# Modulation weights of stage 0 split by GpSimd, with products issued two pieces behind

## The chip, the cores and the metric
One core of one Trainium2 chip (trn2). The metric is the device time of one launch in microseconds (us), the median of the runs shown. TensorE is called PE, its weight loads PEld, VectorE DVE, ScalarE ACT, GpSimd POOL, SyncE SP, as in the profile; a q behind a name is that engine's instruction queue.

## The reference, cut to what matters
One step of a small diffusion backbone on 512 latent and 128 context tokens of width 1024, in fp32. Layer 0 mixes by pooling, layer 1 by retention; each is followed by an MLP. Every sub-layer has a norm with shift, scale and gate that come from the conditioning vectors:

```python
mod = (jax.nn.silu(cond) @ w_ada[i] + b_ada[i])[:, None, :]
sh_a, sc_a, g_a, sh_m, sc_m, g_m = jnp.split(mod, N_MOD, axis=-1)
h = rmsnorm(x, norm_mix_w[i]) * (1 + sc_a) + sh_a
mix = pool_mixer(h, pool_w[j], pool_b[j], pool_scale[j], grid)
x = x + g_a * mix
h = rmsnorm(x, norm_mlp_w[i]) * (1 + sc_m) + sh_m
x = x + g_m * sq_relu_mlp(h, mlp_w1[i], mlp_w2[i])
```

`cond` has two rows here (c for the latent tokens, c_ctx for the context), so that a modulation is a product of 2 vectors of 1024 with a 1024x1024 matrix: 4 MB of weights for few multiplications.

## The kernel before
All tokens stand side by side as 640 columns, with the features on partitions (`xall`, eight tiles of 128 features). An fp32 matmul with full accuracy is made of three faster ones: each operand is split into a high part `hi` of type fp32r and the rest `lo` (`split`, line 144: ACT casts `hi`; line 145: a TENSOR_TENSOR subtracts, on DVE unless `sub` names another engine), and `mm3` (lines 205 to 207) adds hi*hi, hi*lo and lo*hi.

**Stage 0** is layer 0 up to its MLP. Five of layer 0's six modulations are made in it, in the order 1, 0, 2, 4, 3 (`ada`, called with `MODES`). A modulation has eight pieces, two halves of 512 columns with four pieces of 256 rows each; so there are 40, and piece 17 is the first of modulation 2, 25 the first of 4, 33 the first of 3. Two pieces come by one DMA of 1 MB into a `wst` buffer. The letter of `MODES` says how a piece is taken:
- `p`: whole; two fp32 products on PE (line 283, `ps<-wst,c`; each is two MATMUL records of the profile), straight from the `wst` buffer;
- `v`: split, the low part on DVE; four fp32r products (`ps<-whi,chl` and `ps<-wlo,chl`);
- any other letter (`g`): split, the low part on POOL.

`LAG` is how many pieces the products stand behind: `queue` holds the pieces that are split and not yet multiplied, and `issue` takes the oldest once more than `LAG` are in it. When a half is complete, line 287 copies the sum from PSUM (ACT), line 293 turns it by transposes on PE, line 294 adds it up on DVE (`mod`), and lines 304 and 414 finish the modulation. `PLAN` says after which step of the other work how many pieces are taken. That other work is:
- `pooled(d)` for eight feature tiles: transposes (621, 622), window sums (630, 632), the scaled token n (637, ACT), the difference df (638 and 639, DVE: 638 reads PSUM and `iv`, 639 reads df and n), its split into `h{d}h` and `h{d}l` (144 ACT, 145 DVE). For every second d, `group` splits four token tiles (`t<-xt`), makes `pm` (601) and loads `iv` (596, on ACT's queue);
- line 659: x gets the bias of the pooling (ACT, 16 pieces of work); it needs modulation 2;
- the pool adds, `pool_add(n, h)`: six matmuls with the split pool weights (two `whi`/`wlo` pairs, which stay in use until the end), `xall` (line 500, DVE), the square (435, ACT) and its sum (447 DVE, or 455 PE);
- the norm ahead of the MLP: `rsqrt` (lines 150 to 159, DVE) for each half of the tokens, then line 487 (DVE) and 489 (ACT), which give the first operand of the MLP's first matmul.

`whi` and `wlo` have four buffers each, for the pieces, the pool weights and the MLP's weights. The order on each engine is set by a scheduler when the kernel is built; each engine then runs its queue in order.

Of the kernel before, what the change touches and what calls it, by code (L numbers as in the profile page):

```python
# [46 lines left out]

MODES = ("pvvv vvvv", "vvvv vvvv", "vpvp vpvp", "ppvp ppvp", "ppvp ppvp")  # L50
MODE5 = "s s"
PLAN = ("a2 l a4 v a5 a5 w0 a2 w1 a2 w2 a2 w3 a2 w4 a2 w5 a2 w6 a2 w7",
        "a1", "a1", "a1", "a1", "a1", "a1", "a1", "a1")
LAG = 1
FIRST = "x x x x x"
LATE = (False, True)
TURN = 5
# [53 lines left out]
def hybrid_kernel(ctx: ExitStack, tc: tile.TileContext, x_prompt, x_sample, state_ret, c, c_ctx, w_ada, b_ada,  # L111
# [6 lines left out]
    def nm(s):  # L118
        uid[0] += 1
        return f"{s}_{uid[0]}"  # L120
# [280 lines left out]
    def stepper(gen):  # L401
        def step(n=1, until=None):
            while n if until is None else until not in ready:
                try:
                    next(gen)
                except StopIteration:
                    return
                n -= 1
        return step
# [141 lines left out]
    with tc.tile_pool(name="pool", bufs=1) as pp:  # L551
        extra[:] = [(wst, 2), (pp, 3), (pp, 3), (wst, 2), (pp, 3)]
        win_sb = pp.tile([128, W_N], F32, name="win_sb")
        room[1] = lambda: pp.tile([128, 1024], F32, tag="acc", name=nm("acc"), bufs=1)
        astep = stepper(ada([(0, m, modes) for m, modes in zip((1, 0, 2, 4, 3), MODES)], LAG))

# [689 lines left out]
```

## Time and profile before

| what | us |
|---|---|
| median of 3 runs (1621.11 to 1624.91) | 1624.71 |
| the profiled execution | 1622.77 |
| its span, first to last instruction | 1621.0 |
| busy in the span: PE, PEld | 1582.8 (98%), 1473.6 (91%) |
| busy in the span: DVE, ACT, POOL | 1164.0 (72%), 727.0 (45%), 11.7 (1%) |
| granted clock of PE, mean | 0.994 |

The busy time of an engine is the union of its instructions. A matmul's time includes its way through the array, so that matmuls in a row overlap: how long a piece holds PE is read from start to start. "idle before" is idle time of the engine just ahead of an instruction, with what ended it. A stretch of the span says more than the whole: the first 122 us are stage 0.

### The profile page before, as it was taken

The page shows a single profiled execution, that of the slowest core. Times are in us where ns is not written, and L with a number is a line of the kernel's source. Part 1 is how long each engine was busy: PE and PEld are TensorE (multiplying, and loading weights), DVE is VectorE, ACT ScalarE, POOL GpSimd, SP SyncE. Part 2 cuts the span into 40 slices and gives each one's busy share as a digit, 9 for nine tenths or more (in the row PEclk, how much of TensorE's full clock was granted, in tenths as well). Part 3 has the DMA queues.
Part 4 walks back from the last instruction along what each step waited for, and adds up shares of the span by engine and source line. Part 5 has one row for each costly group of instructions (what it writes and reads, how often), then busy time and mean ns, then how long its engine had stood idle before and what let it go on. Part 6 is the DMA issues. An engine that isn't in the chain of part 4 may idle for free. (4 is left out here: it accounts for less than half of the span.)

```text
span 1621.0 us, 24493 instructions
## 1 busy us (share of the span) xinstructions
PE 1582.8 (98%) x9897; PEld 1473.6 (91%) x9897; DVE 1164.0 (72%) x2254; ACT 727.0 (45%) x1338; POOL 11.7 (1%) x26
## 2 busy tenths in 40 slices
PE   6999999999999999999999999999999999999997
PEld 3459999999999988889889988998899999999997
DVE  6879996676766687886797678778967573554654
ACT  6747326336156354433442443353464371451640
POOL 0000000000000000000000000000000000000000
PEclk9999999999999999999999999999999999999999
DMA  9744333333314123323304241322032132131221
GB/s 356 252 141 146 105 105 104 104 124 111 105 53 156 45 70 128 96 79 130 128 29 156 63 146 64 118 92 91 26 105 79 34 124 78 53 104 53 95 75 66
DMA packets 137954, 169.83 MB, mean 105 GB/s; under 512 B 3512, under 2 KB 111472, under 8 KB 137840
## 3 DMA queue, kind: packets, MB, share of 16 engines
q1 hardware_dynamic: 134800, 161.28, 30.2%
q0 software_dynamic: 1312, 4.20, 0.8%
q10 hardware_dynamic: 1728, 2.78, 0.5%
q8 instruction: 78, 1.28, 0.3%
q14 instruction: 36, 0.29, 0.1%
HBM read 161.43 MB, written 6.82 MB: 104 GB/s over the span
## 5 line engine op out<-in xcount | busy, mean ns | idle before, releaser
L144 ACT CAST whi<-wst 128x1024 fp32r<-128x1024 f32 x245 | 254.4, 1049 | 422.5 <-PE ps L206 200.8
L145 DVE TENSOR_TENSOR wlo<-wst,whi 128x1024 fp32r<-128x1024 f32 x245 | 297.3, 1223 | 136.5 <-ACT whi L144 124.0
L205 PE MATMUL ps<-a,whi 128*128 128x320 f32 x896 | 277.2, 310 | 1.2 <-ACT a L144 1.2
L206 PE MATMUL ps<-a,whi 128*128 128x320 f32 x896 | 277.3, 310 | 0.1
L207 PE MATMUL ps<-a,wlo 128*128 128x320 f32 x896 | 276.2, 309 | 0.0
L500 DVE SCALAR_TENSOR_TENSOR xall<-ps,mod,xall 128x320 f32<-128x320 f32 (+2 forms) x288 | 115.7, 436 | 151.6 <-PE ps L207 150.4
L206 PEld LDWEIGHTS ps<-a,whi 128*128 128x128 f32 x896 | 168.2, 188 | 2.1 <-DVE a L145 1.7
L205 PEld LDWEIGHTS ps<-a,whi 128*128 128x128 f32 x896 | 167.9, 188 | 1.8 <-ACT a L144 1.7
L207 PEld LDWEIGHTS ps<-a,wlo 128*128 128x128 f32 x896 | 168.0, 188 | 0.0
L389 DVE SCALAR_TENSOR_TENSOR acc<-wst,c,acc 128x256 f32<-128x256 f32 x336 | 137.6, 483 | 0.0
L205 PE MATMUL ps<-tq,whi 128*128 128x320 f32 x288 | 89.0, 309 | 0.0
L206 PE MATMUL ps<-tq,whi 128*128 128x320 f32 x288 | 89.0, 309 | 0.0
L207 PE MATMUL ps<-tq,wlo 128*128 128x320 f32 x288 | 89.0, 309 | 0.0
L206 PE MATMUL ps<-A,whi 128*128 128x320 f32 x256 | 78.9, 309 | 0.0
L205 PE MATMUL ps<-A,whi 128*128 128x320 f32 x256 | 78.9, 312 | 0.0
L207 PE MATMUL ps<-A,wlo 128*128 128x320 f32 x256 | 78.2, 309 | 0.0
L145 DVE TENSOR_TENSOR a<-t,a 128x320 fp32r<-128x320 f32 x128 | 61.8, 488 | 22.7 <-ACT a L144 22.2
L435 ACT ACTIVATE t<-xall 128x320 f32<-128x320 f32 x56 | 26.0, 471 | 81.2 <-DVE xall L500 81.2
L852 ACT ACTIVATE t<-t 128x320 f32<-128x320 f32 x128 | 60.5, 473 | 1.8
L144 ACT CAST a<-t 128x320 fp32r<-128x320 f32 x128 | 58.5, 457 | 1.5
L207 PEld LDWEIGHTS ps<-tq,wlo 128*128 128x128 f32 x288 | 54.1, 188 | 0.0
L205 PEld LDWEIGHTS ps<-tq,whi 128*128 128x128 f32 x288 | 54.1, 188 | 0.0
(406 smaller groups left out, 4004.4 us busy)
## 6 DMA issues: line engine op xcount, KB each, us to landing
wst<-in_mlp_w_dram SPq DMA_DIRECT2D x64, 1024.0 KB, 5.3
wst<-in_w_ada_dram SPq DMA_DIRECT2D x46, 1024.0 KB, 6.0
wst<-in_ret_w_in_dram SPq DMA_DIRECT2D x24, 1024.0 KB, 5.2
wst<-in_ret_w_out_dram SPq DMA_DIRECT2D x8, 1024.0 KB, 5.0
t<-in_state_ret_dram SPq DMA_DIRECT2D x16, 256.0 KB, 5.5
out_dram<-t POOLq DMA_DIRECT2D x16, 256.0 KB, 2.9
xt<-in_x_sample_dram SPq DMA_DIRECT2D x4, 512.0 KB, 4.8
both<-in_w_ada_dram SPq DMA_DIRECT2D x2, 1024.0 KB, 7.3
```

The source lines that it names most:

```text
L144: S.copy(hi, src)
L145: sub.tensor_tensor(lo, src, hi.bitcast(F32), ALU.subtract)
L205: T.matmul(out, wh, ah, start=first, stop=False, skip_group_check=more)
L206: T.matmul(out, wh, al, start=False, stop=False, skip_group_check=more)
L207: T.matmul(out, wl, ah, start=False, stop=last, skip_group_check=more)
L389: V.scalar_tensor_tensor(acc[j], w[:, k], by, acc[j], ALU.mult, ALU.add)
L435: S.activation(sq[:, o:o + t.shape[-1]], t, AF.Square)
L500: V.scalar_tensor_tensor(x, ps[:, cols], gate[:, d, j:j + 1], x, ALU.mult, ALU.add)
L852: S.activation(f, r, AF.Square)
```

## The change
Two constants. In the last three modulations the letter `p` becomes `g` at twelve of 24 places, and `LAG` goes from 1 to 2.

```diff
-MODES = ("pvvv vvvv", "vvvv vvvv", "vpvp vpvp", "ppvp ppvp", "ppvp ppvp")
+MODES = ("pvvv vvvv", "vvvv vvvv", "vgvg vgvg", "gpvg gpvg", "gpvg gpvg")
-LAG = 1
+LAG = 2
```

The code that reads them is the same in both kernels:

```python
w = [w] if mode == "p" else split_w(w, V if mode == "v" else G)
queue.append(((i, m, q), (pa, w, c4 if mode == "p" else chl, 2 * p, p == 0, p == 3)))
if len(queue) > lag:
    issue()
```

The scheduler orders stage 0 anew; on SP nothing moves, and behind the beginning of the MLP the rows are the same on every engine. Three places:

ACT, where the first pooled tile (d = 0) is made. `wst` and `whi` are a piece's weights and its high part, `h0h` and `h1h` the high parts of df. Before:
```order
L637 ACTIVATE n_451<-ps_435,mod_0_99,a_416 128x128
L144 CAST whi_507<-wst_505 128x1024
L144 CAST h0h_459<-df_452 128x640
L637 ACTIVATE n_492<-ps_475,mod_0_99,a_416 128x512
L637 ACTIVATE n_492<-ps_476,mod_0_99,a_416 128x128
L144 CAST whi_572<-wst_570 128x1024
L596 DMA iv_627<-in_inv_dram 128x640
L144 CAST h1h_500<-df_493 128x640
L287 COPY t_513<-ps_392 4x512
```
Now:
```order
L637 ACTIVATE n_461<-ps_445,mod_0_99,a_426 128x128
L144 CAST whi_473<-wst_409 128x1024
L144 CAST whi_484<-wst_482 128x1024
L637 ACTIVATE n_509<-ps_492,mod_0_99,a_426 128x512
L144 CAST h0h_469<-df_462 128x640
L144 CAST whi_521<-wst_482 128x1024
L637 ACTIVATE n_509<-ps_493,mod_0_99,a_426 128x128
L287 COPY t_529<-ps_388 4x512
L144 CAST whi_533<-wst_531 128x1024
```
Four casts of weights stand where two stood, and the load of the third `iv` has gone to a later row.

POOL behind its first instructions. Before, the next thing on it is the store of a state of layer 1:
```order
L734 IOTA npos 128x896
L736 IOTA ipos 128x512
L737 IOTA ipos 128x512
L739 IOTA ppos 128x1
L740 IOTA ppos 128x1
L1021 DMA out_dram<-t_6540 128x512
```
Now twelve subtractions come first, the first five here:
```order
L739 IOTA ppos 128x1
L740 IOTA ppos 128x1
L145 TENSOR_TENSOR wlo_400<-wst_389,whi_399 128x1024
L145 TENSOR_TENSOR wlo_474<-wst_409,whi_473 128x1024
L145 TENSOR_TENSOR wlo_522<-wst_482,whi_521 128x1024
L145 TENSOR_TENSOR wlo_593<-wst_531,whi_592 128x1024
L145 TENSOR_TENSOR wlo_604<-wst_601,whi_603 128x1024
```
Eight of the twelve belong to pieces whose products stand ahead of the pool adds on PE.

DVE at the end of stage 0: `rstd_1054` (now `rstd_1137`) is the first half's norm, `rstd_1222` (now `rstd_1294`) the second's. Before:
```order
L157 TENSOR_TENSOR t_1053<-rstd_1054 128x320
L294 TENSOR_REDUCE mod_3_102<-ps_1096 128x8
L158 SCALAR_TENSOR_TENSOR t_1053<-t_1053,ps_1051 128x320
L304 TENSOR_TENSOR mod_3_102<-mod_3_102,vec 128x16
L159 SCALAR_TENSOR_TENSOR rstd_1054<-t_1053,rstd_1054 128x320
L150 TENSOR_SCALAR rstd_1222<-ps_1075 128x320
L487 SCALAR_TENSOR_TENSOR t_1121<-xall,a_1103,rstd_1054 128x320
```
Now:
```order
L157 TENSOR_TENSOR t_1136<-rstd_1137 128x320
L150 TENSOR_SCALAR rstd_1294<-ps_1158 128x320
L158 SCALAR_TENSOR_TENSOR t_1136<-t_1136,ps_1134 128x320
L151 TENSOR_SCALAR rstd_1294<-rstd_1294 128x320
L159 SCALAR_TENSOR_TENSOR rstd_1137<-t_1136,rstd_1137 128x320
L487 SCALAR_TENSOR_TENSOR t_1193<-xall,a_1175,rstd_1137 128x320
```
The end of modulation 3 (`mod_3`) is gone from here to an earlier place, and the second half's L150 stands ahead of three steps of the first.

## Rows read from the trace of the kernel before

**Rows 1.** Stretches: start and end, length, busy time (instructions) of each engine, PEclk.
```profile
core 0: us, PE busy (x) PEld busy (x) DVE busy (x) ACT busy (x) POOL busy (x), PEclk, DMA share, GB/s
42.50:84.60 42.10, 41.94 (x195) 22.26 (x195) 34.75 (x68) 34.08 (x65) 0.00 (x0) 1.00 0.71 240
42.50:92.00 49.50, 49.34 (x222) 25.14 (x223) 41.56 (x80) 38.10 (x71) 0.00 (x0) 1.00 0.72 241
86.50:122.40 35.90, 34.32 (x159) 20.56 (x158) 27.27 (x61) 14.75 (x27) 0.00 (x0) 1.00 0.44 139
122.40:1621.00 1498.60, 1476.06 (x9420) 1417.23 (x9420) 1070.24 (x2076) 648.11 (x1209) 8.71 (x16) 1.00 0.29 93
```
**Rows 2.** Timeline around the first pool add: start, length, engine, line, operation.
```profile
83.55 1.04 ACT L144 CAST whi<-wst 128x1024 fp32r<-128x1024 f32 x1
...
86.54 0.41 PE L205 MATMUL ps<-h0h,whi 128*128 128x320 f32 x1
```
**Rows 3.** Timeline of PE, a split piece and a whole one.
```profile
93.62 0.40 PE L283 MATMUL ps<-whi,chl 128*4 128x512 f32 x1
...
94.55 0.31 PE L205 MATMUL ps<-h2h,whi 128*128 128x320 f32 x1
...
95.53 1.88 PE L283 MATMUL ps<-wst,c 128*4 128x512 f32 x4
97.34 0.41 PE L205 MATMUL ps<-h4h,whi 128*128 128x320 f32 x1
```
**Rows 4.** Groups of ACT, 42.5 to 86.5: busy us, mean ns, idle before.
```profile
L637 ACT ACTIVATE n<-ps,mod,a 128x512 f32<-128x512 f32 (+1 forms) x16 | 9.9, 618 | 4.6 <-PE ps L632 2.9 <-PE ps L621 1.6
L144 ACT CAST whi<-wst 128x1024 fp32r<-128x1024 f32 x9 | 9.3, 1037 | 0.1
L659 ACT ACTIVATE xall<-xall,gb 128x512 f32<-128x512 f32 (+1 forms) x16 | 7.9, 554 | 0.0
```
**Rows 5.** Groups of POOL in the whole span.
```profile
L734 POOL IOTA npos<- 128x896 int16 x1 | 0.9, 917 | 0.1
```
**Rows 6.** Timeline, the end of stage 0.
```profile
117.49 0.58 ACT L287 COPY t<-ps 4x512 f32<-4x512 f32 x1 [1.30 <-PE ps L283]
...
118.94 1.88 PE L455 MATMUL ps<-t,ones_d 128*128 128x320 f32 x6
...
119.14 0.48 DVE L158 SCALAR_TENSOR_TENSOR t<-t,ps 128x320 f32<-128x320 f32 x1
...
120.86 0.49 DVE L150 TENSOR_SCALAR rstd<-ps 128x320 int32<-128x320 int32 x1 [0.72 <-PE ps L455]
...
121.84 0.56 ACT L489 ACTIVATE h0h<-t,mod 128x320 fp32r<-128x320 f32 x1 [3.78 <-DVE t L487]
...
122.46 0.41 PE L205 MATMUL ps<-h0h,whi 128*128 128x320 f32 x1 [1.64 <-ACT h0h L489]
```
**Rows 7.** Groups of DVE, 42.5 to 92.
```profile
L145 DVE TENSOR_TENSOR wlo<-wst,whi 128x1024 fp32r<-128x1024 f32 x10 | 12.2, 1219 | 0.7 <-ACT whi L144 0.7
L638 DVE SCALAR_TENSOR_TENSOR df<-ps,a,iv 128x512 f32<-128x512 f32 (+1 forms) x16 | 8.6, 549 | 4.2 <-PE ps L630 3.4 <-ACT n L637 0.6
L639 DVE SCALAR_TENSOR_TENSOR df<-df,mod,n 128x512 f32<-128x512 f32 (+1 forms) x16 | 8.5, 548 | 0.2
L145 DVE TENSOR_TENSOR t<-xt,t 128x256 fp32r<-128x256 f32 x16 | 6.1, 419 | 0.4 <-ACT t L144 0.4
...
L145 DVE TENSOR_TENSOR h1l<-df,h1h 128x640 fp32r<-128x640 f32 x1 | 0.8, 821 | 0.0
```
**Rows 8.** DMA issues, 0 to 200: KB each, median us to landing.
```profile
iv<-in_inv_dram ACTq DMA_DIRECT2D x4, 320.0 KB, 5.4
```
**Rows 9.** Stretches before stretch A, columns as in rows 1.
```profile
14.00:20.00 6.00, 1.98 (x5) 0.28 (x4) 4.67 (x14) 4.85 (x7) 0.00 (x0) 0.94 1.06 388
20.00:26.00 6.00, 4.31 (x10) 1.17 (x11) 6.00 (x7) 4.08 (x5) 0.00 (x0) 0.50 1.05 389
```

## The prediction
> **What bounds the kernel now.** I read the stretches of the span first, then one piece's matmuls, then ScalarE (ACT), VectorE (DVE) and GpSimd (POOL) in the same stretches, then the tail. Look in [rows 1] for the stretch in which TensorE (PE) is never free. From 42.5 to 84.6 us, where the pooled features are made and pieces 17 to 32 are multiplied (stretch A; it ends with the first pool-weight matmul at 86.54 [rows 2]), PE is busy 41.94 of 42.10 us, ACT 34.08. From 86.5 to 122.4 (stretch B: the pool adds, pieces 33 to 40, the start of the MLP's norm) PE is busy 34.32 of 35.9, and from 122.4 to the end 1476.06 of 1498.6. So PE is the bound in all three, and a microsecond by which the MLP's first matmul at 122.46 [rows 6] moves is a microsecond of the total. Such a read says what a lighter PE can give; what it can get depends on who is nearly as full. In A that is ACT (81%) and DVE.
>
> **What the change does, part by part.** 12 of the 17 whole pieces become split ones; POOL gets 12 subtractions and ACT 12 casts. DVE's and SP's work stays as it is, and no row on SP moves.
>
> *PE, per piece.* A whole piece runs from 95.53 to the next matmul at 97.34, 1.81 us; a split one from 93.62 to 94.55, 0.93 [rows 3]. Saving 0.88. In A eight pieces change (four of 17 to 24, four of 25 to 32): -7.0 us. In B four: -3.5 us.
>
> *ACT in A.* Eight casts of 1.04 us, about 1.0 each back to back [rows 4]: +8.0. In the new order the cast of h7h (0.7) and the last L637 (0.5) also stand ahead of the first pool-weight cast, which ended at 83.55 + 1.04 = 84.59 [rows 2]. So ACT has 34.1 + 8.0 + 1.2 = 43.3 us to do where it had 42.1 us of time: with no idle at all the cast ends at 42.5 + 43.3 = 85.8. That alone eats PE's 7.0: the pool adds begin at 85.8 where they began at 86.5. Reading lesson: the saving is on the full engine, but its load goes to one with only 8.0 us free.
>
> *POOL, one subtraction.* No row shows one. Nearest row: the IOTA, 128x896 in 0.917 us [rows 5], so 1.05 us for 1024 elements that are only written. An end from above: two operands read in turn and one written, three such passes, 3.1 us; from below 1.05. DVE does the same subtraction in 1.22 [rows 7]. I take two passes, 2.1 us: POOL's own row is the nearest, and the IOTA reads nothing where this reads two. By the Trainium skill's GPSIMD Engine Reference, Performance versus the Vector engine, 4497 ns for 2048 fp32 elements, an estimate would be 2.25 us, and the sum below would be 1.2 us more; no run here shows it yet.
>
> *DVE beside POOL, the largest term.* Eight subtractions stand before the pool adds: 16.8 us. DVE's order there has, up to the last L639 of d = 7: t 6.1, L639 8.5, L638 8.6, h lows 7 x 0.82 = 5.7, five wlo 6.1, the two pm and the smallest groups of that view 3.7 [rows 7], 38.7 us. One instruction begins before the last has ended: in the view the groups add to 47.1 us where the stretch counts 41.56 [rows 1], factor 0.88, so 34.2. Beginning at 43.2 it is through at 77.4. Behind it ACT has h7h (0.7), eight L659 (half of 7.9) and the cast (1.04), 5.7 us, so that DVE may be as late as 85.8 - 5.7 = 80.1 and costs nothing: slack 2.7. Now the unknown. L638 has one operand in PSUM and takes 549 ns; L639 has both in SBUF and takes 548: DVE reads a second SBUF operand at no cost. Whether it can do so while POOL reads two, no row shows. Ends: side by side, 0; one after the other, all 16.8 us on DVE's queue but for what DVE can do meanwhile with a PSUM operand, about one L638 per subtraction, 8 x 0.55 = 4.4. I take the second end: 16.8 - 4.4 = 12.4, less the slack 2.7, is 9.7 past 85.8. Why: the widest that the rows show is DVE's two reads beside ACT's one, and nothing in them speaks for four streams. DVE is in order, so what is queued behind a held L145 or L639 (the next df, h and t) waits, then ACT's h casts, then the L659 and the pool weights. The trace of before has no POOL read, so this rests on a choice. The Trainium skill, SBUF — State Buffer, SBUF: two separate sides, states that a DVE instruction with two SBUF inputs and a GpSimd one that reads SBUF exclude each other for the whole instruction; by it the sum is the one I take, and without it the first rival's. It speaks against this change.
>
> Stretch A: pool adds at 85.8 + 9.7 = 95.5 against 86.5, **+9.0**.
>
> *Stretch B.* PE -3.5. The last two pieces now stand ahead of the last pool adds, so nothing of them is left in the tail; but the copy L287 of their result stands on ACT behind two MLP casts, of which the second waits for the buffer that the last piece frees, and PE's transposes L293 wait in order behind it: 1.04 + 0.58 [rows 4, 6], +1.6. In the tail, PE's sums L455 end at 120.82 and DVE's L150, L487, ACT's L489 lead to PE at 122.46, 1.6 us. The new order puts the second norm's L150 ahead of L158 of the first, so that L158, L151 and L159 (0.48 each or less [rows 6]) come behind the last sum too: +1.3. POOL's last four subtractions lie beside 35.9 us in which DVE has 27.27; I cost them at nothing (end: 4 x 2.1). Sum -0.6. Two of the four iv loads on ACT's queue now stand only some 5 us of DVE rows ahead of their L638; they land in 5.4 [rows 8], so I cost them at nothing, at most 1 us each.
>
> Products two pieces behind: PE's order before the pooling has one split piece more ahead of the turn of mod 0; ACT had 0.7 us idle there; nothing.
>
> Sum: +9.0 - 0.6 = **+8.4 us**. The profiled execution took 1622.77 (span 1621.0 and 1.8 around it): 1631.2. It lies 1.9 under the median of the runs, 1624.71, so I forecast **1633.1**. With POOL at 1.05 us A is +0.6 and all is as before; with 3.1 A is +17.0, total 1641.1.
>
> **The rivals.**
> 1. *POOL runs beside DVE.* Then ACT sets A: -0.7, and B -0.6: 1623.4. For it: POOL is empty (11.7 us in the span) and DVE would have its slack of 2.7. Decides: an L145 or L639 of unchanged time while POOL subtracts.
> 2. *Faster: PE's saving is kept.* POOL beside DVE, no wait at L293 and the tail as it was: B -3.5, and A -0.7 or, if the casts overlap their neighbours better than by 0.88, -2: 1619.2 at best. Against it: ACT's 43.3 us of work. Decides: ACT idle in A of 5 us or more and PE still full.
> 3. *PE grows slow.* PE would stand idle a quarter of A. Early in this trace, after PE's idle time to 20 us, the granted clock is 0.50 from 20 to 26 us, its level of 1.2 GHz [rows 9]. In A PE waits anyway; in B (some 30 us of matmuls) half a stretch at that level would cost 10 us or more beyond the forecast, 1643. Or the subtraction takes over 3.1 us, with the same end.
> That the change does not do what it says is excluded by the order: twelve TENSOR_TENSOR rows stand on POOL, and behind stage 0 no row moves.
>
> **How the numbers follow.** A change under 0.3% (4.9 us) can't be told from none here. Forecast 0.60, rival 1 0.25, rival 2 0.10, rival 3 0.05. Of the forecast 0.05 lies within 0.3% (a cheap subtraction); of rival 1 0.24 does, 0.01 gains more; rival 2's end of -5.5 counts as faster. Faster 0.11, same 0.29, slower 0.60. The range takes in rival 1 with its small waits gone (1621) and the upper price (1642), and leaves out rival 2 and 3.
>
> **What would show it.** Right: in A DVE's L145 and L639 stretched (or a POOL subtraction far above 2.1), ACT waiting for DVE at the h casts, PE idle 15 us or so, the first L205 at about 95; the MLP's first matmul at about 131; behind it the same length as before. Wrong: L145 at 1.22 beside a busy POOL (rival 1), or first L205 before 84 (rival 2). If A is longer but PE waits for whi and not for what DVE makes, ACT was it and not POOL.

## The result, and the profile after

The changed kernel takes **1639.36 us** (median of 4 runs, 1638.31 to 1642.06) against 1624.05 for the kernel before beside it (1621.11 to 1624.91): 15.3 us more, ratio 1.0102 with a 95% interval of 1.0088 to 1.0116. The profiled execution is the slowest of the four, 1642.06, with a span of 1640.3. It is 2.7 us above its median and the profiled execution of before 1.9 below, so that the two traces differ by 19.3 us where the medians differ by 15.3.

Three marks tell where it went. The first pool add moved from 86.54 [rows 2] to 101.47, 14.9 later. The MLP's first matmul moved from 122.46 [rows 6] to 141.17, 18.7 later. The span is 19.3 longer. So 14.9 us, about four fifths, were lost ahead of the pool adds (stretch A), 3.8 behind them (stretch B), and 0.6 in the other 1500 us.

Stretches of the changed kernel, columns as in [rows 1]:
```profile
42.50:101.47 58.97, 43.10 (x199) 25.11 (x197) 50.50 (x72) 41.49 (x74) 24.06 (x9) 0.88 0.56 191
101.47:108.00 6.53, 6.53 (x22) 4.28 (x23) 6.26 (x7) 3.73 (x5) 2.06 (x1) 0.55 0.47 144
108.00:124.00 16.00, 13.78 (x67) 7.21 (x65) 11.07 (x16) 8.50 (x13) 5.05 (x3) 1.00 0.24 74
124.00:128.00 4.00, 4.00 (x18) 4.00 (x18) 2.58 (x8) 0.82 (x2) 0.00 (x0) 0.57 0.56 177
128.00:141.17 13.17, 10.37 (x57) 8.59 (x55) 12.39 (x32) 5.60 (x12) 0.00 (x0) 1.00 0.27 85
```
PE, which was never free in stretch A [rows 1], is now idle 15.9 of 59.0 us there. DVE is now the fullest engine, 50.5 of 59.0, though the change gave it no work. Its groups in that stretch (busy us, mean ns, idle before):
```profile
L639 DVE SCALAR_TENSOR_TENSOR df<-df,mod,n 128x128 f32<-128x128 f32 (+1 forms) x16 | 13.5, 858 | 0.2
L145 DVE TENSOR_TENSOR t<-xt,t 128x256 fp32r<-128x256 f32 x16 | 12.1, 784 | 0.5 <-ACT t L144 0.5
L638 DVE SCALAR_TENSOR_TENSOR df<-ps,a,iv 128x128 f32<-128x128 f32 (+1 forms) x16 | 8.6, 546 | 3.1 <-PE ps L630 2.9 <-DMA iv<-in_inv_dram 0.2
L145 DVE TENSOR_TENSOR h3l<-df,h3h 128x640 fp32r<-128x640 f32 x1 | 2.8, 2809 | 0.1
L145 DVE TENSOR_TENSOR h5l<-df,h5h 128x640 fp32r<-128x640 f32 x1 | 2.6, 2579 | 0.1
```
GpSimd's group, from 42 to 101:
```profile
L145 POOL TENSOR_TENSOR wlo<-wst,whi 128x1024 fp32r<-128x1024 f32 x9 | 24.5, 2736 | 60.7 <-ACT whi L144 53.2 <-PE ps L283 7.6
```
Beside [rows 7]: L639 from 8.5 to 13.5, t from 6.1 to 12.1, two h lows from 0.8 each to 2.8 and 2.6. That is 14.8 us more on DVE. L638, which reads PSUM, is as it was. PE is slower as well in stretch A: its granted clock is 0.88 there, and its busy time is 43.1 us, where the same matmuls in the same order take 36.8 at 0.97 in run e2 below. The timeline of GpSimd, and then of DVE, shows the holding itself (start, length):
```profile
105.94 2.38 POOL L145 TENSOR_TENSOR wlo<-wst,whi 128x1024 fp32r<-128x1024 f32 x1 [16.58 <-DVE mod L294]
...
116.86 2.36 POOL L145 TENSOR_TENSOR wlo<-wst,whi 128x1024 fp32r<-128x1024 f32 x1 [1.90 <-ACT whi L144]
```
```profile
106.12 2.23 DVE L414 SCALAR_TENSOR_TENSOR a<-mod,vec 128x16 f32<-128x16 f32 x1
...
117.33 0.55 DVE L500 SCALAR_TENSOR_TENSOR xall<-ps,ga,xall 128x320 f32<-128x320 f32 x1 [0.34 <-PE ps L207]
```
L414 has 16 columns and took 0.17 us before; here it ends at 108.35, when GpSimd's 105.94 + 2.38 = 108.32 is over. L500 at 117.33, which reads PSUM and one SBUF operand, stands in the middle of the next GpSimd subtraction (to 119.22) and takes its usual 0.55. So these instructions take turns; neither runs at a slower pace.

Who waited, in the groups of PE from 42.5 to 141 (the first column behind the bar is busy time, the numbers behind the second bar are idle time):
```profile
L630 PE MATMUL ps<-pm,t 128*128 128x512 f32 (+3 forms) x64 | 18.4, 421 | 4.9 <-DVE t L145 4.9
L283 PE MATMUL ps<-wlo,chl 128*4 128x512 f32 x40 | 16.9, 424 | 5.0 <-POOL wlo L145 3.5 <-DVE wlo L145 1.5
L293 PE MATMUL ps<-tab_sb,t 4*128 4x4 f32 x28 | 3.0, 210 | 1.8 <-ACT t L287 1.8
L205 PE MATMUL ps<-h0h,whi 128*128 128x320 f32 x4 | 2.2, 552 | 6.9 <-ACT whi L144 6.9
```
The 6.9 us are the end of the chain. DVE's L639 came late, ACT waited 3.78 us for it at the cast of h6, then had h7h, the L659 and the pool weights' casts still to do while PE stood still. The length of this last wait does not measure the contention: in e2, where nothing is held, PE waits 7.8 us for the same cast. What moved is its place, 14 us later.
```profile
92.55 0.72 ACT L144 CAST h6h<-df 128x640 fp32r<-128x640 f32 x1 [3.78 <-DVE df L639]
...
96.77 3.72 ACT L659 ACTIVATE xall<-xall,gb 128x512 f32<-128x512 f32 x8
100.39 1.98 ACT L144 CAST whi<-wst 128x1024 fp32r<-128x1024 f32 x2
```

### The profile page after: what moved, and what is told of

Same layout as the page of the kernel before. It is cut to its first block, busy times and chain, and to the rows that moved or that the text cites. A ratio compares the mean times of both kernels' runs of the same rounds, so it can differ in the third digit from the quotient of the medians.

```text
span 1640.3 us, 24545 instructions
## 1 busy us (share of the span) xinstructions
PE 1582.7 (96%) x9897; PEld 1481.5 (90%) x9897; DVE 1183.3 (72%) x2254; ACT 737.0 (45%) x1350; POOL 43.3 (3%) x38
## 4 chain that ended last, share of the span: by engine, by line
PE 77%; DVE 6%; ACT 5%; DMA 3%; issue 1%; DVEq 0%; SPq 0%; ACTq 0%
PE ps L205 23%; PE ps L206 23%; PE ps L207 23%; DMA wst<-in_mlp_w_dram 3%; PE ps L992 2%; PE ps L991 2%; PE ps L990 2%; ACT whi L144 2%; DVE wlo L145 1%; DVE acc L389 1%; PE ps L394 1%; PE ps L465 0%; ACT t L483 0%; ACT t L851 0%; ACT t L852 0%
## 5 line engine op out<-in xcount | busy, mean ns | idle before, releaser
L144 ACT CAST whi<-wst 128x1024 fp32r<-128x1024 f32 x257 | 265.8, 1047 | 430.7 <-PE ps L206 209.1
L500 DVE SCALAR_TENSOR_TENSOR xall<-ps,mod,xall 128x320 f32<-128x320 f32 (+2 forms) x288 | 115.7, 436 | 150.8 <-PE ps L207 149.8
L205 PE MATMUL ps<-h0h,whi 128*128 128x320 f32 x148 | 47.2, 326 | 9.7 <-ACT whi L144 6.9
```

The source lines that it names most:

```text
L144: S.copy(hi, src)
L205: T.matmul(out, wh, ah, start=first, stop=False, skip_group_check=more)
L500: V.scalar_tensor_tensor(x, ps[:, cols], gate[:, d, j:j + 1], x, ALU.mult, ALU.add)
```

## The experiments

Three theories. **Contention**: a GpSimd subtraction and a DVE instruction with two SBUF operands hold each other up. **Casts and order**: ACT's twelve casts and the new order (LAG 2) make the loss, GpSimd is a bystander. **Late low parts**: PE waits because GpSimd begins only behind ACT's cast. The ratios are to the kernel before, run beside each, and comparisons between runs go by them; the marks are of one profiled execution each, up to about 4 us from its median.

| run | ratio (95%) | first pool add | MLP's first matmul |
|---|---|---|---|
| changed kernel | 1.0102 (1.0088 to 1.0116) | 101.47 | 141.17 |
| e1_dve | 1.0042 (1.0025 to 1.0059) | 84.40 | 127.61 |
| e2_set | 1.0022 (1.0012 to 1.0032) | 87.12 | 125.00 |
| e3_copy | 1.0023 (1.0014 to 1.0032) | 89.31 | 125.42 |
| e4_g_early | 1.0092 (1.0077 to 1.0107) | 97.86 | 137.37 |
| e5_const | 1.0102 (1.0077 to 1.0127) | 98.65 | 137.25 |
| e6_g_late | 1.0007 (0.9995 to 1.0018) | 86.47 | 121.78 |
| e7_lag1 | 1.0069 (1.0053 to 1.0084) | 89.88 | 136.42 |
| e8_lag2 | 1.0017 (1.0008 to 1.0027) | 86.36 | 124.16 |
| f1_v_late | 0.9991 (0.9982 to 1.0000) | 85.25 | 119.40 |
| f2_gcast | 0.9989 (0.9979 to 0.9999) | 84.65 | 120.17 |
| f3_g_late1 | 0.9997 (0.9988 to 1.0006) | 86.81 | 121.70 |
| f4_v_late1 | 0.9979 (0.9970 to 0.9987) | 85.16 | 118.09 |

**e1: DVE in GpSimd's place.**
```diff
-"vgvg vgvg", "gpvg gpvg", "gpvg gpvg"
+"vvvv vvvv", "vpvv vpvv", "vpvv vpvv"
```


> The changed kernel with its twelve subtractions on DVE instead of GpSimd (g to v); casts, LAG 2 and the pieces stay. Theory one (a GpSimd subtraction and a DVE instruction that reads two SBUF operands hold each other up): DVE gets 12 x 1.22 us and loses the stretch of some 14.6 us that its L639, t and h lows show before the pool adds; DVE has then 36.7 + 9.8 = 46.5 us there, so the first pool add comes at 89 to 95 and not 101.5, L639 takes 0.35 or 0.75 everywhere, and the time is 1626 to 1632 us. Theory two (the twelve casts on ACT and the new order with LAG 2 make the loss, GpSimd is a bystander): DVE only gets more work, the time stays at 1637 to 1642.

1628.75 us, by the ratios some 10 less than the changed kernel, as contention has it: DVE does the work in less time than it loses by waiting for GpSimd to do it. L639 is back at 549 ns. The order is not kept here: the first pool add came earlier than I gave, at 84.40, and the stretch behind it is longer instead, 43.2 us, with PE waiting 3.55 us for a cast of ACT's at 99.07. So the first pool add is a fair mark only between runs of one order.

**e2: GpSimd only writes.**
```diff
-sub.tensor_tensor(lo, src, hi.bitcast(F32), ALU.subtract)
+G.memset(lo.bitcast(F32), 0.0) if sub is G else sub.tensor_tensor(lo, src, hi.bitcast(F32), ALU.subtract)
```


> The changed kernel, but GpSimd fills each of the twelve low parts with zeros, reading nothing (the low products of these pieces are left out of the sums, PE still multiplies them). The order of the instructions on PE, DVE and ACT is the changed kernel's. Theory one: no DVE instruction is stretched, L639 takes 0.35 or 0.75 us; ACT's 43 us of work bound the stretch, first pool add at 86 to 89, time 1620 to 1627 us. Theory two: the casts and the order are still there, so the first pool add stays at 99 to 102 and the time at 1635 to 1640.

1626.65 us. With each engine's order kept, 13 us of the 15 are gone. Groups of GpSimd (whole span) and of DVE (42.5 to 101):
```profile
L145 POOL MEMSET wlo<- 128x1024 f32 x12 | 11.4, 954 | 85.3 <-PE ps L283 85.3
```
```profile
L639 DVE SCALAR_TENSOR_TENSOR df<-df,mod,n 128x128 f32<-128x128 f32 (+1 forms) x16 | 8.5, 548 | 0.2
```
Casts and order cannot make the loss. They do cancel the gain. The stretches of the kernel before and of this run, up to the first pool add and on to the MLP:
```profile
42.50:86.54 44.04, 43.88 (x200) 22.53 (x200) 36.68 (x71) 35.64 (x68) 0.00 (x0) 1.00 0.70 238
86.54:122.46 35.92, 34.28 (x160) 20.56 (x159) 27.29 (x61) 14.77 (x27) 0.00 (x0) 1.00 0.44 140
```
```profile
42.50:87.10 44.60, 36.84 (x199) 22.86 (x197) 35.77 (x71) 40.94 (x75) 7.23 (x8) 0.97 0.72 251
87.10:125.00 37.90, 33.65 (x158) 23.33 (x158) 28.30 (x60) 18.78 (x31) 2.86 (x3) 0.90 0.33 105
```
PE has 36.8 us to do where it had 43.9, the 7.0 that were forecast, and still the pool adds begin 0.6 later, with PE idle 7.77 us in front of them for ACT's cast.

**e3: GpSimd reads one operand.** As e2, with `G.tensor_copy(lo, src)` for the memset.

> The changed kernel, but GpSimd copies wst into each of the twelve low parts and does not subtract (one SBUF operand read where it was two; these low parts are wrong). The order on PE, DVE and ACT is the changed kernel's. If it is GpSimd's second operand that shuts DVE out: DVE unstretched, time as with the zeros, 1620 to 1627 us. If any SBUF read of GpSimd's does: DVE's L639 and L145 are held for the length of a copy, some 1.0 to 2.0 us each, and the time lies between, 1627 to 1637. Theory two (casts and order): 1635 to 1640.

1625.86 us: the time of the first answer, the rows of the second. GpSimd's copy does hold DVE (the rows are of the whole span and of 42.5 to 101):
```profile
L145 POOL CAST wlo<-wst 128x1024 fp32r<-128x1024 f32 x12 | 13.5, 1131 | 85.3 <-PE ps L283 41.1 <-DMA wst<-in_w_ada_dram 36.5 <-issue 6.5
```
```profile
L639 DVE SCALAR_TENSOR_TENSOR df<-df,mod,n 128x128 f32<-128x128 f32 (+1 forms) x16 | 10.5, 671 | 0.2
```
DVE is busy 40.44 us up to the first pool add, 4.7 more than in e2 (35.77), and the first pool add comes 2.2 later than there. So one operand is enough to hold. That the two marks move by 4.7 and 2.2 fits a hold that costs only what goes beyond DVE's slack (2.7 in the prediction). The stretch behind the pool adds is 1.8 shorter than in e2 in these traces, because PE is busy 1.8 less at a granted clock of 0.96 where e2 had 0.90; so the equal times rest in part on PE's clock.

**e4: only the two early modulations on GpSimd.**
```diff
-"vgvg vgvg", "gpvg gpvg", "gpvg gpvg"
+"vgvg vgvg", "gpvg gpvg", "ppvp ppvp"
```


> The changed kernel with the last modulation's pieces as before (ppvp ppvp): eight pieces on GpSimd before the pool adds, none after; LAG 2. Both theories on the first stretch: first pool add at 99 to 103. They differ on the second: if the four late pieces cost nothing but a saving on PE of 3.5 us that is lost to small waits, the time stays within 1.5 us of the changed kernel (1638 to 1641); if the stretch after the pool adds is longer (39.7 us where it was 35.9) because of the late GpSimd pieces, it goes back to 36 to 37 and the time falls by 3 to 4, to 1635 to 1637.

1637.35 us, between the two answers. The first pool add comes at 97.86: one GpSimd subtraction fewer stands ahead of it, the ninth, which belongs to the last modulation. Behind it the stretch is 39.5 us, as long as in the changed kernel, though no GpSimd work is left there. So the late GpSimd pieces, with what they save on PE and what they make it wait, neither lengthen nor shorten stretch B.

**e5: the same GpSimd work without its wait.** In e2 and e3 GpSimd no longer waited for ACT's cast either, so late low parts were still possible. Here the operation, shape and place stay, and only the operands are other ones.
```diff
-sub.tensor_tensor(lo, src, hi.bitcast(F32), ALU.subtract)
+sub.tensor_tensor(lo, *((src, hi.bitcast(F32)) if sub is V else [win_sb[:, 0:512].unsqueeze(1).to_broadcast([128, 2, 512])] * 2), ALU.subtract)
```


> The changed kernel, but the twelve GpSimd subtractions read a constant table twice (win_sb) in place of wst and whi: the same operation, shape and place, two SBUF operands as before, but no wait for ACT's cast, so that the low part is there early (these low parts are wrong). The order on PE, DVE and ACT is the changed kernel's. Zeros and copies on GpSimd took the wait for ACT away too, so two theories still stand. Contention (GpSimd's reads hold DVE): DVE's L639 and L145 are held as in the changed kernel, some 12 to 15 us in all before the pool adds, first pool add at 95 to 101, time 1632 to 1639. Late low parts (PE waits for GpSimd, which began only behind ACT's cast, and the rest follows): PE never waits for a low part, first pool add at 87 to 90, time 1625 to 1628.

1637.50 us, ratio 1.0102, that of the changed kernel. PE never waited for a GpSimd result, and the loss is the same: the theory of late low parts falls, contention stands. DVE is busy 47.1 us up to the first pool add, where e2 had 35.8 in the same order, although a GpSimd subtraction is shorter here (2.00 us on average). DVE's L639 in that stretch:
```profile
L639 DVE SCALAR_TENSOR_TENSOR df<-df,mod,n 128x128 f32<-128x128 f32 (+1 forms) x16 | 14.5, 922 | 0.2
```
One place of the hold, on GpSimd and on DVE:
```profile
72.94 2.21 POOL L145 TENSOR_TENSOR wlo<-win_sb 128x1024 fp32r<-128x1024 f32 x1 [3.58 <-PE ps L283]
```
```profile
73.30 1.88 DVE L304 TENSOR_TENSOR mod<-mod,vec 128x16 f32<-128x16 f32 x1
```
Two tiles that have nothing to do with each other: L304 (16 columns, 0.17 us elsewhere) ends at 75.18, GpSimd at 75.15.

**e6, e7, e8: the parts alone.** e6 is the kernel before with `gpvg gpvg` as the last modulation and LAG 2; e7 the changed kernel with LAG 1; e8 the kernel before with LAG 2.

> The kernel before with LAG 2 and only the last modulation changed (gpvg gpvg: four pieces on GpSimd, one of them ahead of the pool adds, three behind). Contention: one subtraction of 2.4 to 2.6 ahead of the pool adds, where DVE has 7 us free, costs nothing; behind them DVE has 8.6 us free against 7.1, and PE saves 3.5, of which small waits take some: 1620 to 1625 us. If the late pieces are dear by themselves (their casts and the waits for their buffers): 1626 to 1629.

> The changed kernel with LAG 1 again. If the second part of the change (products two pieces behind) neither helps nor harms, it is within 2 us of the changed kernel, 1637 to 1641. If LAG 2 was what gives GpSimd's longer subtraction time before PE wants its result, PE waits about 1 us more at each of the twelve: 1643 to 1652. If LAG 2 makes the loss, 1625 to 1632.

> The kernel before with LAG 2 alone, the pieces as they were. Contention: there is no GpSimd work, PE is full before the pool adds whichever piece comes first, so 1621 to 1625. If products two pieces behind bring a cost of their own (a sum that comes later, a low part that holds its buffer longer): 1626 to 1630, which would explain part of what the changed kernel loses even where GpSimd reads nothing (1626.65).

e6: 1624.04 us, no difference from before that can be measured. Where DVE has room, four subtractions on GpSimd cost nothing that shows. Its stretch behind the pool adds:
```profile
86.47:121.78 35.31, 30.56 (x160) 20.88 (x159) 33.12 (x62) 19.04 (x32) 8.40 (x3) 1.00 0.44 142
```
e7: 1633.69, by the ratios 5.4 us less than the changed kernel and in none of the three ranges that I gave: LAG 2 harms, but is not the whole loss. LAG 1 also orders the engines anew, and the long wait of PE for a cast of ACT's then stands behind the first pool add, which comes at 89.88:
```profile
100.33 0.59 PE L283 MATMUL ps<-whi,chl 128*4 128x512 f32 x1 [8.99 <-ACT whi L144]
```
e8: 1624.70, by its time in the first range, but the kernel before took 1621.95 beside it: ratio 1.0017 with an interval above 1, a cost of its own of some 2.8 us, which is the second answer's theory. Part of it is in the tail. With LAG 2 DVE has the second norm's L150 ahead of L158, L151 and L159 of the first, which PE waits for:
```profile
121.40 0.49 DVE L150 TENSOR_SCALAR rstd<-ps 128x320 int32<-128x320 int32 x1
121.81 0.48 DVE L158 SCALAR_TENSOR_TENSOR t<-t,ps 128x320 f32<-128x320 f32 x1
122.20 0.32 DVE L151 TENSOR_SCALAR rstd<-rstd 128x320 int32<-128x320 int32 x1
122.44 0.48 DVE L159 SCALAR_TENSOR_TENSOR rstd<-t,rstd 128x320 f32<-128x320 f32 x1
```
PE's idle time ahead of the MLP is 2.79 us here, as in the changed kernel, and was 1.64 [rows 6]. The rest of the 2.8 I have not taken apart.

**f1 to f4: versions with LAG 1, from the kernel before.** f1: last modulation `vpvp vpvp`. f3: `gpvg gpvg`. f4: `vpvv vpvv`. f2 splits three early pieces more, with the cast on GpSimd and the subtraction on DVE:
```diff
-"vpvp vpvp", "ppvp ppvp", "ppvp ppvp"
+"vkvp vkvp", "pkvp ppvp", "ppvp ppvp"
-S.copy(hi, src)
-sub.tensor_tensor(lo, src, hi.bitcast(F32), ALU.subtract)
+G.tensor_copy(hi, src) if sub is G else S.copy(hi, src)
+V.tensor_tensor(lo, src, hi.bitcast(F32), ALU.subtract)
```


> The kernel before (LAG 1) with two more split pieces in the last modulation, both on DVE (vpvp vpvp); the end of the first norm keeps its order. Behind the pool adds PE is full and DVE and ACT are not: PE saves 2 x 0.88 us, DVE pays 2 x 1.22 and ACT 2 x 1.04 out of idle time, so 1 to 2 us (0.06 to 0.12%) less than before. If the small waits (copy L287 behind a cast) take it, no difference.

> The kernel before (LAG 1) with three more split pieces ahead of the pool adds, whose high part GpSimd casts (one operand read) and whose low part DVE subtracts. GpSimd's copy of 1024 columns took 1.04 us and held DVE for no more than that: DVE pays 3 x (1.22 + 1.04) = 6.8 of 7.4 us that it has idle, ACT pays nothing, PE saves 3 x 0.88 = 2.6. If that holds, 1 to 2.5 us less than before. If DVE has no such slack where it is needed (its idle time is waiting for PE), 0 to 3 us more.

> The four late pieces on GpSimd (gpvg gpvg) as in the changed kernel, but with LAG 1, and the other modulations as before. With LAG 2 this was within 0.2% of the kernel before (ratio 1.0007), and LAG 2 alone cost 0.17%; if the two costs simply add, this is 0.05 to 0.15% faster than before (1 to 2.5 us). If with LAG 1 PE waits for GpSimd's 2.4 us at each late piece (a wait that LAG 2 hid), it is 1 to 3 us slower.

> The same four late pieces with DVE in place of GpSimd (vpvv vpvv), LAG 1. DVE pays 4 x 1.22 = 4.9 us of 8.6 idle behind the pool adds, where GpSimd's four subtractions take 4 x 2.4 and hold DVE for up to 9.6. Contention: 0.5 to 2 us less than with GpSimd, 1 to 3 us less than before. If DVE's idle time there lies in waits for PE and not at the casts, no difference to GpSimd.

f4 is the fastest, **1619.36 us, ratio 0.9979 (0.9970 to 0.9987)**, 3.3 us under the kernel before beside it and by the ratios 20 under the changed one. f1 (1620.94) and f2 (1620.69) lie about 0.1% below the kernel before, f2 by an interval that just leaves out 1, f1 by one that ends at it. f3 (1621.47) is the kernel before again. f3 and f4 split the same four pieces, and differ in who subtracts: behind the pool adds GpSimd's take 2.42 us each and PE waits 1.9 us for them, DVE's 1.22 and PE waits 0.1. Groups of PE, 42.5 to 126, in f3 and in f4:
```profile
L283 PE MATMUL ps<-wlo,chl 128*4 128x512 f32 x24 | 9.4, 393 | 1.9 <-POOL wlo L145 1.9
```
```profile
L283 PE MATMUL ps<-wlo,chl 128*4 128x512 f32 x24 | 9.4, 393 | 0.1
```

## Why the prediction was right, and where it was off

**The mechanism** was right: DVE's two-operand instructions wait for GpSimd's, ACT for DVE, PE for ACT's last casts, and PE's saving is not seen in the time. e2 and e5 show it from both sides. The Trainium skill (SBUF — State Buffer, SBUF: two separate sides) says that whichever of the two starts first keeps the ports for the whole instruction, and that a DVE instruction with two SBUF inputs meets this only against a GpSimd instruction that reads SBUF; L414 and L304 above, held to GpSimd's end, and e2, where a write alone holds nobody, agree with it. **The size** was too small: +8.4 forecast, 15.3 measured. That 1639 still lies in the range is partly luck, since the range's upper end, 1642, stood for a subtraction of 3.1 us, and what came was a ninth subtraction ahead of the pool adds and a slower PE. Of the signs that were named, PE idle for 15 us in A came (15.9), the first pool add came at 101.47 and not about 95, the MLP's first matmul at 141.17 and not about 131. The last sign, PE waiting for whi if ACT is the cause, does not separate the two: the longest wait is for whi with the contention (6.9) and without it (7.8 in e2).

- *PE's saving in A*, 7.0 us: right (36.84 in e2, 43.88 before).
- *ACT ends at 85.8 at the earliest*: right within a little over 1 us (87.12 in e2), but partly by luck. ACT had 40.9 us of work there and not 43.3, and 3.7 idle where I gave none. The lesson held that the load goes to the next full engine.
- *One GpSimd subtraction*, 2.1 us: too low. Singly it took 2.36 to 2.48; the nine of stretch A took 2.74 on average, because DVE holds GpSimd too. My bounds of 1.05 and 3.1 held. The estimate of 2.25 by the Trainium skill (GPSIMD Engine Reference, Performance versus the Vector engine) was nearer, and low as well.
- *Eight before the pool adds*: nine. I counted pieces by their modulation; the new order has the last modulation's first split piece ahead of them. e4, without it, has the pool adds 3.6 us earlier, about one subtraction and one cast, though PE's granted clock was better there too (0.94). With nine of 2.4 in place of 16.8 my own step gives 85.8 + 21.6 - 4.4 - 2.7 = 100.3, and 101.47 was measured. So these two sizes can carry the miss in A. How much of it PE's lower clock in A adds, which I put at nothing ("In A PE waits anyway"), no run separates.
- *L638 goes on beside GpSimd*: right, 546 ns.
- *Stretch B*, -0.6: wrong, +3.8. The terms that I summed were right, as e6 shows: with the same last modulation and LAG 2, but no long idle stretch of PE ahead, its stretch B is 35.31 us against 35.92, -0.6. In the changed kernel the waits were about as forecast: 1.45 at L293 (1.6), 1.16 more in the tail (1.3), and 0.77 for a low part of GpSimd's that I had at nothing. What I left to rival 3 is the granted clock. Behind PE's 6.9 idle us it is 0.55 from 101.47 to 108, and again 0.57 from 124 to 128, near the level of 1.2 GHz. PE is busy 34.68 us in B where e6 has 30.56 at full clock, 4.1 more. So B is made up of -3.7 saved (30.56 where before had 34.28), 3.4 more idle (5.02 against 1.64) and 4.1 of slower clock. So an idle PE cost more than its idle time; it was not the 10 us I gave.
- *LAG 2 at nothing*: wrong, 0.17% alone (e8), of which I had the tail in B. In the changed kernel it is worth more, 5.4 us by the ratios (e7), though in another order of the engines. It may also be what lifts rival 1, whose mechanism e2 has: 1626.65 where I gave 1623.4.

The runs divide the loss, in ratios: LAG 2 alone 1.0017; with the twelve lighter pieces and no GpSimd read 1.0022; with the reads 1.0102. So, added in this order, some 13 us are the reads with all that follows from them (PE's clock too), about 3 are LAG 2, and the pieces themselves gave nothing, as ACT was the bound. The parts do not simply add: with the reads, LAG 2 costs about twice what it costs alone.

## What to carry to other kernels

Giving a two-operand operation to GpSimd in place of DVE does not free DVE. It takes DVE's two-operand work out for the whole of GpSimd's longer instruction, here 2.4 us for 1.2; if DVE can spare that, it can do the operation itself, as f4 does. Look for the engine that is full in the stretch and for the one that would be next, and count what stands ahead of a mark in the new order, not by the loop's numbers. Give work to engines in the stretch where they have room: four pieces behind the pool adds, split on DVE, gained 0.2% (f4), where twelve lost 0.4% on DVE (e1) and 1% on GpSimd, both with LAG 2.

## What was not expected of the hardware

- The hold is whole and goes both ways: a 16-column DVE instruction took 2.23 us in place of 0.17, and two GpSimd subtractions in a row took 6.29 us in place of 4.8: they begin at 58.71 in the changed kernel, while DVE works from 58.66 on at instructions with two SBUF operands.
- GpSimd's price depends on what it reads: 128x1024 written in 0.95 us, copied in 1.04, subtracted in 2.38, and the same subtraction of one table from itself in 1.89. Only the write left DVE alone.
- PE's granted clock was at about half behind idle stretches of some 7 us: 0.55 for 6.5 us of matmuls in the changed kernel, 0.50 for 3.8 in e2. It fell again at 124, with only 1.45 idle us just ahead; e6 has a wait of 1.44 at the same place, and its clock stayed at 1.00 up to the MLP. What decides between the two is open.
